# Half-array products of samples with turned keys and of the prompt with V, issued in turn on both halves of the columns

## The chip, the cores and the metric

The kernel runs on one core of one Trainium2 chip. The metric is the device time of one execution in microseconds (us). A core has engines with queues of their own, which run beside each other and wait for each other through semaphores: TensorE (PE, matrix products; its weight loads are listed as PEld), VectorE (DVE), ScalarE (ACT), GpSimd (POOL) and SyncE (SP), which here only issues transfers (DMA). TensorE is an array of 128 rows by 128 columns; the stationary operand of a product lies in the array, its columns become the output's partitions. A product with only 64 stationary columns occupies half of the columns: here called a half-array product, on half A (output partitions 0 to 63) or half B (64 to 127).

## The reference

One layer of a decoder for two groups of requests that share all weights: a prompt of 512 tokens (with 16 learned tokens ahead of it) and 8 samples of 8 new tokens, each with 1024 past tokens in a paged cache. Each layer has a state-space branch, a sparse attention branch (16 heads, 4 key/value heads of 64 elements), a gated sum of both, and a two-matrix network. All in float32. The part that matters here, cut down:

```python
def attend_selected(q, k_sel, v_sel, valid):
    qh = q.reshape(b, nq, ATT_KV_HEADS, ATT_GROUP, HEAD_DIM).astype(F32)
    s = jnp.einsum('bqhgd,bqkhd->bqhgk', qh, k_sel.astype(F32)) * HEAD_DIM ** -0.5
    s = jnp.where(valid[:, :, None, None, :], s, -jnp.inf)
    p = jax.nn.softmax(s, axis=-1)
    o = jnp.einsum('bqhgk,bqkhd->bqhgd', p, v_sel.astype(F32))

y_ssm, ssm_new, conv_new = ssm_mixer(...)            # state-space branch
y_att = attend(q, k, v, qi, wi, ki)                  # 128 (prompt) or 256 (samples) best keys
merged = sigmoid(g_ssm) * (y_ssm @ w_ssm_proj) + sigmoid(g_attn) * (y_att @ w_attn_proj)
```

The kernel does not gather the selected keys: it scores all of them and adds a mask that is very negative where a key isn't selected.

## The kernel before, in words

The stages run one after another: the normed input times w_in, with convolution and state-space scan (to about 690 us), the attention of the samples and then of the prompt (about 690 to 953 us), with the product of the state-space branch and w_ssm_proj spread among both (`L1068`), the rest of the merge, and the network. The order in which an engine's instructions stand is not the order of the source: a scheduler with a model of its own of how long things take places them; the source gives what depends on what. On TensorE it puts the products of `L1068`, and later the first of w_attn_proj (`L162`), wherever the attention is not ready. They are called fillers below.

**Samples** (`sample(b)`, 8 of them, each cut into steps by `yield` and run as a pipeline). A gather brings the sample's keys `Kg` and values `Vg` from the pages. TensorE transposes the keys (`L892`), and copies bring them from PSUM (the accumulators' memory) to `KcT`: those of the first pair of heads (hp = 0) by VectorE, those of the second (hp = 1) by ScalarE (`L893`). Then the scores (`L900`): for three stretches of keys (512, 512 and 64), one half-array product with the queries of hp = 0 on half A and one with those of hp = 1 on half B, both into one PSUM buffer `v`. VectorE adds the mask and takes the maximum (`L901`), ScalarE takes the exponential (`L904`), TensorE transposes the probabilities (`L913`, `L916`), and half-array products with V follow (`L923`, `L926`).

**Prompt** (`query(t, hp, gp)`, 16 groups: four blocks t of 128 queries, two pairs of heads hp, two halves gp). Scores (`L1002`, `L1003`), mask and maximum (`L1004`), exponential (`L1007`), scaling (`L1018`), then transposes of the probabilities (`L1024`) and copies into `PT`: of the pair's first head (e = 0) by VectorE, of the second (e = 1) by ScalarE (`L1025`). One step of the pipeline later come the products with V (`L1034`): for each of nk = t + 1 blocks of keys, one half-array product for e = 0 on half A and one for e = 1 on half B, and a full one for the first 16 keys (`L1035`).

A wait that the kernel's framework puts in is of the data: a product of hp = 0 waits for VectorE's copy, one of hp = 1 for ScalarE's. So the scheduler may place an A product as soon as VectorE's copy is expected, and its B later.

Of the kernel before, what the change touches and what calls it, by code (L numbers as in the profile page):

```python
# [1 line left out]

# [1 line left out]

# [66 lines left out]
def body(ctx, tc, a, o):  # L71
    nc = tc.nc
    SB, PS, DR = bass.MemoryType.SB, bass.MemoryType.PSUM, bass.MemoryType.DRAM
    act, dve, pool, pe, sy = nc.scalar, nc.vector, nc.gpsimd, nc.tensor, nc.sync
# [9 lines left out]
    def pst(tag):  # L84
        return psp.tile([128, 512], FT, tag=tag, name=tag, bufs=PSB[tag])

    class Pipe:
# [8 lines left out]
        def run(self, units=()):  # L96
            for u in units:
                self.push(u)
            while self.live:
                self.push()  # L100

    alt = [0]

# [76 lines left out]
    Vt = ap_.tile([128, 6, 256], FT, name="Vt")  # L180
# [45 lines left out]
    for t in range(5):  # L226
# [7 lines left out]
        for q in range(2):  # L234
            ps = mis()
            pv = ps.rearrange("p (k n) -> p k n", k=4)
# [26 lines left out]
    def pieces(n):  # L263
        return [(c, min(c + 512, n)) for c in range(0, n, 512)]
# [49 lines left out]
    with tc.tile_pool(name="p1", bufs=1, reuse_waits="tile") as p1:  # L314
# [26 lines left out]
        pv = ps.rearrange("p (k n) -> p k n", k=4)  # L341
# [202 lines left out]
        for kp in range(8):  # L544
            hp, gi = divmod(kp, 4)
# [312 lines left out]
    with tc.tile_pool(name="p2s", bufs=1, reuse_waits="tile") as p2, \  # L858
            tc.tile_pool(name="p2k", bufs=1, reuse_waits="tile") as p2k:
        qTs = p2.tile([128, 8, 64], FT, name="qTs")  # L860
        sy.dma_start(qTs, d_q[:, :, 512:576].rearrange("k p n -> p k n"))
        QZs = [p2.tile([128, 2, 64], FT, name=f"QZ{i}") for i in range(2)]
        for z in QZs:
            pool.memset(z, 0.0)
        krows = a["cache_k"].rearrange("d n (s e) h c -> (d n s) (e h c)", e=4)
        vrows = a["cache_v"].rearrange("d n (s e) h c -> (d n s) (e h c)", e=4)

        def sample(b):
            QZ = QZs[b % 2]
            for hp in range(2):  # L870
                for e in range(2):
                    src = qTs[64 * e:64 * e + 64, 4 * hp:4 * hp + 4, 8 * b:8 * b + 8]
                    dst = QZ[64 * e:64 * e + 64, hp, 32 * e:32 * e + 32].rearrange("p (g s) -> p g s", s=8)
                    act.copy(dst, src)
            Kg, Vg = [], []
            for lst, name, src in ((Kg, "Kg", krows), (Vg, "Vg", vrows)):
                for q in range(2):
                    lst.append(p2k.tile([128, 1024], FT, tag=name, name=name, bufs=4 if name == "Kg" else 2))
                    pool.indirect_dma_start(out=lst[q], out_offset=None, in_=src,
                                            in_offset=bass.IndirectOffsetOnAxis(ap=idx2[:, b, q:q + 1], axis=0))  # L880
            P = p2.tile([128, 1088], FT, tag="P", name="P", bufs=3)
            sy.dma_start(P,
                         bass.AP(tensor=d_ms.tensor, offset=d_ms.offset + (32 * (b // 2) + 8 * (b % 2)) * 1088,
                                 ap=[[0, 16], [1088, 8], [1, 1088]]))
            KcT = p2.tile([128, 2, 1024], FT, tag="KcT", name="KcT", bufs=2)
            for q in range(2):
                for hp in range(2):
                    dv = KcT[:, hp, :].rearrange("c (p s) -> c s p", s=8)
                    ps = pst("s")
                    pv = ps.rearrange("p (k n) -> p k n", k=4)  # L890
                    for i in range(4):
                        pe.transpose(pv[:, i, :], Kg[q][:, 256 * i + 128 * hp:256 * i + 128 * hp + 128], idf)  # L892
                    (act.copy if hp else dve.tensor_copy)(dv[:, 4 * q:4 * q + 4, :], pv)  # L893
            yield
            mx = p2.tile([128, 12], FT, tag="mxs", name="mxs", bufs=2)
            for c, (c0, c1) in enumerate(pieces(1088)):
                v = pst("s")[:, :c1 - c0]
                for hp in range(2):
                    kk = KcT[:, hp, c0:c1] if c < 2 else KT[:, hp, 528:592]
                    pe.matmul(v[64 * hp:64 * hp + 64], QZ[:, hp, :], kk, start=True, stop=True)  # L900
                dve.tensor_tensor_reduce(P[:, c0:c1], v, P[:, c0:c1], 1.0, NEG, OP.add, OP.max, accum_out=mx[:, c:c + 1])  # L901
            dve.tensor_scalar(mx[:, 3:4], mx[:, 0:1], mx[:, 1:2], None, op0=OP.max)
            dve.tensor_scalar(mx[:, 4:5], mx[:, 3:4], mx[:, 2:3], -0.125, op0=OP.max, op1=OP.mult)
            act.activation(P, P, AF.Exp, scale=0.125, bias=mx[:, 4:5], accum_out=mx[:, 5:6])  # L904
            dve.reciprocal(mx[:, 9:10], mx[:, 5:6])
            yield
            PTs = p2.tile([128, 9, 128], FT, tag="PTs", name="PTs", bufs=1)
            pv_ = P[:, 0:1024].rearrange("r (p s) -> r s p", s=8)
            for q in range(2):
                ps = pst("a")  # L910
                pv = ps.rearrange("p (k n) -> p k n", k=4)
                for i in range(4):
                    pe.transpose(pv[:, i, :], pv_[:, 4 * q + i, :], idf)  # L913
                (act.copy if q else dve.tensor_copy)(PTs[:, 4 * q:4 * q + 4, :], pv)
            ps = pst("a")
            pe.transpose(ps[:64, 0:128], P[:, 1024:1088], idf)  # L916
            act.copy(PTs[:64, 8, :], ps[:64, 0:128])
            py = pst("a")
            for s in range(9):
                for hp in range(2):  # L920
                    h = slice(64 * hp, 64 * hp + 64)
                    if s < 8:
                        pe.matmul(py[h, 0:128], PTs[:, s, h], Vg[s // 4][:, 256 * (s % 4) + 128 * hp:256 * (s % 4) + 128 * hp + 128],  # L923
                                  start=(s == 0), stop=False)
                    else:
                        pe.matmul(py[h, 0:128], PTs[:64, 8, h], Vt[:64, 5, 128 * hp:128 * hp + 128],  # L926
                                  start=False, stop=True)
            on = p2.tile([128, 128], FT, tag="on", name="on", bufs=2)
            dve.tensor_scalar(on, py[:, 0:128], mx[:, 9:10], None, op0=OP.mult)
            yield  # L930
            py = pst("a")
            pe.transpose(py[:, 0:128], on, idf)
            for e in range(2):
                pr = slice(64 * e, 64 * e + 64)
                src = py[pr, 0:128].rearrange("p (h x) -> p h x", h=2)[:, :, 32 * e:32 * e + 32].rearrange(
                    "p h (g s) -> p h g s", s=8)
                h_, l_ = [y[pr, :, 512 + 8 * b:520 + 8 * b].rearrange("p (h g) s -> p h g s", h=2) for y in (yah, yal)]
                act.activation(h_, src, AF.Copy)
                dve.tensor_tensor(l_, src, h_.bitcast(FT), op=OP.subtract)

        Pipe().run(sample(b) for b in range(8))
    p4s_stack = ctx.enter_context(ExitStack())
    p4s = p4s_stack.enter_context(tc.tile_pool(name="p4s", bufs=1, reuse_waits="tile", side="right"))
    with tc.tile_pool(name="p2h", bufs=1, reuse_waits="tile", side="right") as p2h, \
# [6 lines left out]
        for kv in range(4):  # L951
            hp, e = divmod(kv, 2)
# [13 lines left out]
        def query(t, hp, gp):  # L966

            L, nk = LT[t], t + 1
# [24 lines left out]
            PT = p2.tile([128, 2, 4, 2, 128], FT, tag="PT", name="PT", bufs=2)  # L993
            PR = p2.tile([96, 256], FR, tag="PR", name="PR", bufs=2)
            for g in range(2):
                P2 = p2q.tile([128, 2, 528], FT, tag="P", name="P2", bufs=3)
                mx = p2q.tile([128, 2, 6], FT, tag="mx", name="mx", bufs=4)
                for e in range(2):
                    lq = QS[:, 2 * gp + g, e, :]
                    for i, (c0, c1) in enumerate(cuts):  # L1000
                        v = pst("s")[:, :c1 - c0]
# [18 lines left out]
                for e in range(2):  # L1020
                    ps = pst("a")
                    pv = ps.rearrange("p (k n) -> p k n", k=4)
                    for j in range(nk):
                        pe.transpose(pv[:, j, :], P2[:, e, 128 * j:128 * j + 128], idf)  # L1024
                    (act.copy if e else dve.tensor_copy)(PT[:, e, :nk, g, :], pv[:, :nk, :])  # L1025
                pr_ = pst("a")
                pe.transpose(pr_[:96, 0:128], flat(ts).bitcast(FT), idf)
                act.copy(PR[:, 128 * g:128 * g + 128], pr_[:96, 0:128])
# [1 line left out]
            py = pst("s")  # L1030
            for j in range(nk):
                for e in range(2):
                    kv = 64 * (2 * hp + e)
                    pe.matmul(py[64 * e:64 * e + 64, 0:256], Vt[:, j, kv:kv + 64], PT[:, e, j], start=(j == 0), stop=False)  # L1034
            pe.matmul(py[:, 0:256], VZ[:, 128 * hp:128 * hp + 128], PR, start=False, stop=True)  # L1035
            k0 = 4 * hp + 2 * gp
            pv = py[:, 0:256].rearrange("p (g n) -> p g n", g=2)
            h_ = yah[:, k0:k0 + 2, 128 * t:128 * t + 128]
            act.activation(h_, pv, AF.Copy)
            dve.tensor_tensor(yal[:, k0:k0 + 2, 128 * t:128 * t + 128], pv, h_.bitcast(FT), op=OP.subtract)  # L1040

        Pipe().run(query(t, hp, gp) for t in range(4) for hp in range(2) for gp in range(2))

    HALVES = ((0, HQ), (HQ, NQ))
# [404 lines left out]
```

## Time and profile before

| | us |
|---|---|
| median of 3 runs (lowest to highest) | 1459.08 (1458.08 to 1460.82) |
| profiled execution | 1461.18 |
| its span, first to last instruction | 1459.4 |
| TensorE busy | 1422.9 (97%) |
| VectorE busy | 1091.1 (75%) |
| ScalarE busy | 754.3 (52%) |

A record of TensorE begins when the product begins to stream and ends when its last result is out, so records that follow each other overlap, and the sum of their durations is more than the time they took. What a group of records took is read from start to start, or from the union of their busy time in a window. Every float32 half-array product is listed as two records.

### The profile page before, as it was taken

What the parts mean: (1) busy time and instruction counts of PE and PEld (TensorE: products, weight loads), DVE (VectorE), ACT (ScalarE), POOL (GpSimd) and SP (SyncE); (2) the same over time, 40 slices, a digit from 0 to 9 for tenths busy, and PEclk for the clock granted to TensorE, in tenths of its full rate; (3) what the DMA queues carried; (4) which work ended last, traced back from release to release, by engine and by line L of the source; (5) the groups of instructions that cost most, each with busy time, mean ns of one, the idle gap of its engine ahead of it and who ended that gap; (6) DMA issues with size and microseconds to landing.
All of it is one profiled execution on the core that took longest, in us unless ns stands there. A gap on an engine that the chain in (4) does not pass through costs nothing.

```text
span 1459.4 us, 26586 instructions
## 1 busy us (share of the span) xinstructions
PE 1422.9 (97%) x9808; PEld 1271.7 (87%) x9808; DVE 1091.1 (75%) x2248; ACT 754.3 (52%) x1719; POOL 327.0 (22%) x479
## 2 busy tenths in 40 slices
PE   7999999999999999999999999999999999999998
PEld 6998999988987988889688988898798988888986
DVE  6799989999769676572645777765589887878775
ACT  5553365556655664343655777732364554435441
POOL 2110011337445345252422633100000000000001
PEclk9999999999999999999999999999999999999999
DMA  7334375787987878767974533235223222332322
GB/s 199 92 80 117 113 219 152 219 243 209 273 238 199 257 225 235 224 180 248 310 221 128 156 87 86 69 104 177 80 87 102 88 88 85 87 89 87 89 70 73
DMA packets 249340, 222.07 MB, mean 152 GB/s; under 512 B 39325, under 2 KB 212241, under 8 KB 249186
## 3 DMA queue, kind: packets, MB, share of 16 engines
q1 hardware_dynamic: 243962, 201.50, 47.7%
q0 software_dynamic: 5248, 18.88, 3.8%
q8 instruction: 77, 1.26, 0.4%
q14 instruction: 53, 0.43, 0.1%
HBM read 175.50 MB, written 44.07 MB: 150 GB/s over the span
## 4 chain that ended last, share of the span: by engine, by line
PE 83%; DMA 8%; DVE 4%; ACT 2%; POOL 1%; issue 1%; SPq 0%; POOLq 0%; DVEq 0%; ACTq 0%
PE w L162 27%; PE s L1203 15%; PE w L1068 7%; PE a L1329 6%; PE w L1329 4%; PE a L162 3%; DMA bc<-d_ac 2%; PE s L900 2%; PE s L1034 2%; PE a L1203 2%; PE s L763 2%; DMA st<-in_state_ssm_dram 1%; DMA out_dram<-st 1%; PE s L775 1%; PE a L1024 1%; PE a L923 1%
## 5 line engine op out<-in xcount | busy, mean ns | idle before, releaser
L162 PE MATMUL w<-uh,wh 128*128 128x288 f32 (+1 forms) x1168 | 355.4, 304 | 8.4 <-ACT tg L301 2.8
L162 PE MATMUL w<-ul,wh 128*128 128x288 f32 (+1 forms) x1168 | 352.8, 302 | 1.7 <-DVE ul L242 1.7
L162 PE MATMUL w<-uh,wl 128*128 128x288 f32 (+1 forms) x1168 | 353.9, 303 | 0.0
L162 PEld LDWEIGHTS w<-uh,wh 128*128 128x128 f32 x1168 | 222.1, 190 | 15.7 <-ACT tg L301 3.3
L162 PEld LDWEIGHTS w<-ul,wh 128*128 128x128 f32 x1168 | 221.9, 190 | 4.5 <-DVE ul L242 1.9
L162 PEld LDWEIGHTS w<-uh,wl 128*128 128x128 f32 x1168 | 221.2, 189 | 2.6 <-issue 1.9
L123 DVE TENSOR_TENSOR wl<-wr,wh 128x1024 fp32r<-128x1024 f32 x129 | 158.9, 1233 | 78.2 <-ACT wh L122 77.0
L122 ACT ACTIVATE wh<-wr 128x1024 fp32r<-128x1024 f32 x129 | 135.7, 1057 | 143.8 <-PE w L162 81.7
L1205 DVE TENSOR_TENSOR h<-h,s 128x512 f32<-128x512 f32 (+1 forms) x161 | 108.3, 679 | 58.7 <-PE s L1203 58.4
L1203 PE MATMUL s<-dh,hh 128*128 128x512 f32 (+1 forms) x302 | 119.0, 394 | 0.0
L1203 PE MATMUL s<-dl,hh 128*128 128x512 f32 (+1 forms) x302 | 118.7, 393 | 0.0
L172 POOL TENSOR_TENSOR rs<-rs,cst 128x1 f32<-128x1 f32 (+2 forms) x15 | 9.3, 617 | 417.4 <-DVE rs L171 417.2
L1203 PE MATMUL s<-dh,hl 128*128 128x512 f32 (+1 forms) x242 | 95.0, 392 | 0.0
L1068 PE MATMUL w<-ysh,wh 128*128 128x288 f32 x256 | 78.2, 308 | 0.2 <-DVE ms L1073 0.2
L122 ACT ACTIVATE dh<-wr 128x1024 fp32r<-128x1024 f32 x38 | 39.8, 1057 | 73.2 <-PE s L1203 59.3
L1068 PE MATMUL w<-ysh,wl 128*128 128x288 f32 x256 | 77.2, 302 | 0.0
L1068 PE MATMUL w<-ysl,wh 128*128 128x288 f32 x256 | 76.6, 300 | 0.0
L750 ACT ACTIVATE bc<-bc,acum 128x128 f32<-128x128 f32 (+1 forms) x160 | 48.9, 380 | 52.1 <-DMA bc<-d_ac 46.5
L612 DVE SCALAR_TENSOR_TENSOR ca<-rb,cwT,ca 128x616 f32<-128x616 f32 x72 | 69.5, 967 | 0.2
L1203 PEld LDWEIGHTS s<-dl,hh 128*128 128x128 f32 x302 | 56.6, 188 | 12.5
L1203 PEld LDWEIGHTS s<-dh,hh 128*128 128x128 f32 x302 | 56.7, 188 | 10.2 <-DVE h L1205 0.5
L762 DVE SCALAR_TENSOR_TENSOR bc<-bc,dts,cb 128x128 f32<-128x128 f32 (+1 forms) x160 | 54.1, 402 | 0.2
(492 smaller groups left out, 3702.9 us busy)
## 6 DMA issues: line engine op xcount, KB each, us to landing
wr<-in_w_in_dram SPq DMA_DIRECT2D x26, 1024.0 KB
wr<-in_w_up_dram SPq DMA_DIRECT2D x32, 512.0 KB
wr<-in_w_down_dram SPq DMA_DIRECT2D x32, 512.0 KB
st<-in_state_ssm_dram SPq DMA_DIRECT2D x16, 512.0 KB
bc<-d_ac SPq DMA_DIRECT2D x32, 256.0 KB
out_dram<-st SPq DMA_DIRECT2D x16, 512.0 KB
wr<-in_w_ssm_proj_dram SPq DMA_DIRECT2D x16, 512.0 KB
wr<-in_w_in_dram SPq DMA_DIRECT2D x12, 512.0 KB
```

The source lines that it names most:

```text
L122: act.activation(hi, raw, AF.Copy)
L123: (lo_eng or dve).tensor_tensor(lo, raw, hi.bitcast(FT), op=OP.subtract)
L162: pe.matmul(ps[:, :c1 - c0], p[:, k, :], x[:, c0:c1], start=(k == 0 and i == 0), stop=(k == 7 and i == 2))
L612: dve.scalar_tensor_tensor(ca[:, 0:616], rb[:, k:k + 616], cwT[:, 24 * k + ct:24 * k + ct + 1], ca[:, 0:616], op0=OP.mult, op1=OP.add)
L750: act.activation(bc[:n, i, :n], bc[:n, i, :n], AF.Relu, scale=-1.0, bias=acum[:n, c, h0 + i:h0 + i + 1])
L762: dve.scalar_tensor_tensor(mt, mt, dts[:n, c, 8 * g + hh:8 * g + hh + 1], cb[:n, :n], op0=OP.mult, op1=OP.mult)
L763: pe.matmul(py[64 * (hh % 2):64 * (hh % 2) + 64, 128 * (hh // 2):128 * (hh // 2) + n], xt[:n, 64 * hh:64 * hh + 64], mt, start=True, stop= ...
L900: pe.matmul(v[64 * hp:64 * hp + 64], QZ[:, hp, :], kk, start=True, stop=True)
L1068: pe.matmul(ps[:, :HQ], p[:, k, mc], x[k][:, c0:c1], start=(k == 0 and i == 0), stop=(k == 3 and i == 2))
L1203: pe.matmul(ps, p, w[:, cc], start=(k == 0 and i == 0), stop=(k == len(ws) - 1 and i == len(terms) - 1))
L1205: dve.tensor_tensor(h2[:, t, cc], h2[:, t, cc], ps, op=OP.add)
L1329: pe.matmul(ps, p[:, k, :], q[:, k, :], start=(k == 0 and j == 0), stop=(k == 3 and j == 2))
```

## The change

The program's products, copies and sizes stay as they are. For the products of `L900` (now `L906`) and `L1034` (now `L1044`), each one after the first is placed behind the one before it in source order (`issue_after`), so they stand on TensorE in the order A B A B; other instructions may still stand between them. And the first of each group gets a wait for the last copy (ScalarE's) beside the one it has for VectorE's (`needs`).

```diff
+    def needs(ins, other):
+        tc.add_manual_dep(ins, other.name, mybir.DependencyInfo(mybir.DependencyClass.Sync, mybir.DependencyReason.DATA), reason="pair")
...
-                    (act.copy if hp else dve.tensor_copy)(dv[:, 4 * q:4 * q + 4, :], pv)
+                    copied = (act.copy if hp else dve.tensor_copy)(dv[:, 4 * q:4 * q + 4, :], pv)
...
                 for hp in range(2):
                     kk = KcT[:, hp, c0:c1] if c < 2 else KT[:, hp, 528:592]
-                    pe.matmul(v[64 * hp:64 * hp + 64], QZ[:, hp, :], kk, start=True, stop=True)
+                    with tc.issue_after(mm.ins) if c + hp else nullcontext():
+                        mm = pe.matmul(v[64 * hp:64 * hp + 64], QZ[:, hp, :], kk, start=True, stop=True)
+                    if c + hp == 0:
+                        needs(mm.ins, copied.ins)
...
-                    (act.copy if e else dve.tensor_copy)(PT[:, e, :nk, g, :], pv[:, :nk, :])
+                    copied = (act.copy if e else dve.tensor_copy)(PT[:, e, :nk, g, :], pv[:, :nk, :])
...
-                    pe.matmul(py[64 * e:64 * e + 64, 0:256], Vt[:, j, kv:kv + 64], PT[:, e, j], start=(j == 0), stop=False)
+                    with tc.issue_after(mm.ins) if j + e else nullcontext():
+                        mm = pe.matmul(py[64 * e:64 * e + 64, 0:256], Vt[:, j, kv:kv + 64], PT[:, e, j], start=(j == 0), stop=False)
+                    if j + e == 0:
+                        needs(mm.ins, copied.ins)
```

TensorE's order before, at the scores of the fourth sample. The names carry buffer numbers: `s_8955` is the PSUM buffer of the first 512 keys, `s_8959` of the second, `s_8963` of the last 64; in each buffer the first row listed is half A, the second half B. `L1068` are fillers.

```order
L900 MATMUL s_8955<-KcT_8886,QZ1_8621 64x512
L900 MATMUL s_8959<-KcT_8886,QZ1_8621 64x512
L1068 MATMUL w_10985<-ysh_10915,wh_10939 128x288
L1068 MATMUL w_10985<-ysl_10916,wh_10939 128x288
L1068 MATMUL w_10985<-ysh_10915,wl_10938 128x288
L1068 MATMUL w_10985<-ysh_10921,wh_10939 128x288
L1068 MATMUL w_10985<-ysl_10922,wh_10939 128x288
L900 MATMUL s_8955<-KcT_8886,QZ1_8621 64x512
L900 MATMUL s_8959<-KcT_8886,QZ1_8621 64x512
L900 MATMUL s_8963<-KT_76,QZ1_8621 64x64 x2
```

The same sample after (`L906` is the line that was `L900`, `L931` and `L934` the products with V of the sample before it, `L1080` the fillers):

```order
L1080 MATMUL w_11005<-ysh_10933,wh_11001 128x288
L906 MATMUL s_8955<-KcT_8886,QZ1_8621 64x512 x2
L906 MATMUL s_8959<-KcT_8886,QZ1_8621 64x512
L931 MATMUL a_8933<-Vg_8781,PTs_8917 64x128 x8
L931 MATMUL a_8933<-Vg_8783,PTs_8917 64x128 x8
L934 MATMUL a_8933<-Vt_77,PTs_8917 64x128 x2
L906 MATMUL s_8959<-KcT_8886,QZ1_8621 64x512
L906 MATMUL s_8963<-KT_76,QZ1_8621 64x64 x2
```

The two halves of the first buffer now stand together; of the second buffer A stands ahead of the products with V and B behind them. In six of the eight samples all six products stand in a row; the fourth, shown here, and the sixth are cut like this.

TensorE's order before, at one group of the prompt with t = 1 (`PT_9996` holds its probabilities, `L1024` and `L1027` transpose those of the next group, `L1035` closes the group):

```order
L1034 MATMUL s_10194<-PT_9996,Vt_77 64x256
L1068 MATMUL w_11831<-ysl_11744,wh_11825 128x288
L1068 MATMUL w_11831<-ysh_11743,wl_11824 128x288
L1068 MATMUL w_11831<-ysh_11749,wh_11825 128x288
L1068 MATMUL w_11831<-ysl_11750,wh_11825 128x288
L1024 MATMUL a_10133<-cst_66,P2_10091 128x128 x3
L1024 MATMUL a_10138<-cst_66,P2_10091 128x128 x3
L1027 MATMUL a_10143<-cst_66,ts_10108 96x128
L1034 MATMUL s_10194<-PT_9996,Vt_77 64x256 x3
L1035 MATMUL s_10194<-PR_9997,VZ_9746 128x256
```

The same group after (`L1044` is the line that was `L1034`, `L1047` was `L1035`):

```order
L1032 MATMUL a_10133<-cst_66,P2_10091 128x128 x3
L1080 MATMUL w_11863<-ysh_11749,wh_11825 128x288
L1080 MATMUL w_11863<-ysl_11750,wh_11825 128x288
L1080 MATMUL w_11863<-ysh_11749,wl_11824 128x288
L1032 MATMUL a_10138<-cst_66,P2_10091 128x128 x3
L1044 MATMUL s_10194<-PT_9996,Vt_77 64x256 x4
L1010 MATMUL s_10230<-KS_9433,QS_10081 128x400
L1035 MATMUL a_10143<-cst_66,ts_10108 96x128
L1047 MATMUL s_10194<-PR_9997,VZ_9746 128x256
```

The group's first product has moved behind the fillers and transposes, to the other three. The fillers stand in other places all through both attention stages; up to the first sample's scores and from the last group of the prompt on, TensorE's order is the same.

## Rows read from the trace of the kernel before

**Rows 1.** The page: busy time, share of the span and instructions of TensorE.

```profile
PE 1422.9 (97%) x9808; PEld 1271.7 (87%) x9808; DVE 1091.1 (75%) x2248; ACT 754.3 (52%) x1719; POOL 327.0 (22%) x479
```

**Rows 2.** Windows over the attention stages; the first line names the columns.

```profile
core 0: us, PE busy (x) PEld busy (x) DVE busy (x) ACT busy (x) POOL busy (x), PEclk, DMA share, GB/s
700.00:720.00 20.00, 19.38 (x157) 13.94 (x157) 11.62 (x31) 13.76 (x29) 9.42 (x9) 1.00 0.95 312
780.00:800.00 20.00, 20.00 (x174) 16.65 (x171) 8.96 (x23) 10.26 (x21) 6.19 (x7) 1.00 0.47 140
...
920.00:940.00 20.00, 20.00 (x156) 17.85 (x155) 15.45 (x60) 16.11 (x38) 3.48 (x16) 1.00 0.22 67
940.00:960.00 20.00, 18.92 (x143) 15.94 (x142) 10.88 (x37) 12.44 (x30) 2.43 (x12) 1.00 0.13 38
```

**Rows 3.** Waits of TensorE, 716 to 944 us: us in total, times, longest.

```profile
PE w L1068 <- DVE ms L1073: 0.2, 1, 0.2
```

**Rows 4.** Groups by line, TensorE, 683 to 953 us: busy us, mean ns, idle before.

```profile
L1068 PE MATMUL w<-ysh,wh 128*128 128x288 f32 x256 | 78.2, 308 | 0.2 <-DVE ms L1073 0.2
...
L1034 PE MATMUL s<-PT,Vt 128*64 128x256 f32 x160 | 28.2, 391 | 0.6 <-DVE yal L1040 0.3 <-DVE PT L1025 0.2
```

**Rows 5.** Windows of line L1034 alone: us, PE busy (records), PEld, clock, DMA.

```profile
822.00:823.00 1.00, 0.64 (x2) 0.19 (x2) 1.00 0.00 0
856.00:858.00 2.00, 1.08 (x6) 0.47 (x6) 1.00 0.68 187
940.00:943.00 3.00, 1.95 (x16) 1.06 (x16) 1.00 0.01 3
```

**Rows 6.** Timeline of TensorE at a lone product: start us, length us, instruction.

```profile
854.79 0.65 PE L1034 MATMUL s<-PT,Vt 128*64 128x256 f32 x2
855.37 0.41 PE L1068 MATMUL w<-ysh,wh 128*128 128x288 f32 x1
```

**Rows 7.** Timeline of TensorE at two fillers.

```profile
788.12 0.30 PE L1068 MATMUL w<-ysh,wh 128*128 128x288 f32 x1
788.26 0.29 PE L1068 MATMUL w<-ysl,wh 128*128 128x288 f32 x1
```

**Rows 8.** Windows of line L900 alone, one for each sample, columns as in rows 5.

```profile
694.00:699.00 5.00, 3.45 (x12) 1.34 (x12) 1.00 0.88 293
701.00:707.00 6.00, 3.95 (x12) 1.22 (x12) 1.00 0.96 349
713.00:717.00 4.00, 2.34 (x12) 1.45 (x12) 1.00 0.93 343
724.00:731.00 7.00, 3.98 (x12) 1.22 (x12) 1.00 0.79 291
737.00:746.00 9.00, 4.14 (x12) 1.19 (x12) 1.00 0.90 274
753.00:762.00 9.00, 4.47 (x12) 1.31 (x12) 1.00 0.69 211
768.00:772.00 4.00, 3.12 (x12) 0.95 (x12) 1.00 0.24 82
779.00:788.00 9.00, 4.57 (x12) 1.20 (x12) 1.00 0.16 48
```

**Rows 9.** Timeline at the first sample: its first scores, ScalarE's last copy.

```profile
695.09 2.05 PE L900 MATMUL s<-KcT,QZ 128*64 128x512 f32 x5 [0.83 <-DVE KcT L893]
695.33 1.11 ACT L893 COPY KcT<-s 128x512 f32<-128x512 f32 x1
```

**Rows 10.** Timeline of ScalarE: a copy of the largest PT.

```profile
949.00 0.59 ACT L1025 COPY PT<-a 128x512 f32<-128x512 f32 x1
```

**Rows 11.** Timeline of TensorE at the fourth sample's B products.

```profile
727.68 0.64 PE L900 MATMUL s<-KcT,QZ 128*64 128x512 f32 x1
727.69 0.33 PE L900 MATMUL s<-KT,QZ 128*64 128x64 f32 x2
728.16 1.45 PE L900 MATMUL s<-KcT,QZ 128*64 128x512 f32 x3
```

More of the change, by code (lines that the diff above doesn't have):

```diff
@@ L1 @@
-from contextlib import ExitStack
+from contextlib import ExitStack, nullcontext
 import numpy as np
```

## The prediction, made before the changed kernel had run

> **What bounds the kernel now.** I read the page first: TensorE (PE) is busy 97% of the span [rows 1]. Then the table of windows over the two attention stages, about 695 to 953 us: from 780 to 940 us PE is busy for the whole of each 20 us shown, at full clock (1.00), while VectorE and ScalarE have 3.9 to 11 us of every 20 free; only at either end (700 to 720, 940 to 960) is there a gap [rows 2]. The reader is to see there that a microsecond of PE work saved between 716 and 944 us is a microsecond of the kernel, unless another engine is late. The list of waits says the same: in those 228 us PE itself waited 0.2 us for anybody [rows 3]. What it does meanwhile is seen in the groups by line: 768 products of the SSM projection (L1068, in three forms of 256), which need nothing of the attention and fill every hole, and among them the half-array products, of L1034 (prompt probabilities with V, 160 records) [rows 4] and of L900 (scores of samples). Record lengths overlap, so I price by windows of one line's union of busy time, and by start to start, not by mean lengths.
>
> **What a half-array product costs alone, and in a pair.** Every fp32 half-array product shows as two records. Two records by themselves take 0.64 us, six (one pair, one product alone) 1.08, and sixteen (eight products, four pairs, issued A B A B) 1.95 [rows 5]. From 1.08 to 1.95 lie ten records. If a slot holds either a pair or one product alone, the six records are two slots and the sixteen four: (1.95 - 1.08) / 2 = 0.435 us a slot, and 0.64 + 0.435 = 1.08 fits. So a pair takes what one product takes: the two halves of the columns run side by side at full speed, in this very kernel. A product that stands alone between full-array work costs 855.37 - 854.79 = 0.58 us from its start to the start of the next instruction [rows 6]; the 0.15 over a slot is the way in and out. A filler product takes 788.26 - 788.12 = 0.13 to 0.14 us [rows 7].
>
> **Part 1, prompt with V (L1034, 16 query groups).** Before, in 11 of the 16 groups (4 of t = 0, 4 of t = 1, 3 of t = 2) the scheduler has put the first A product some instructions ahead of its B. The piece of PE's order for one group of t = 1 shows it: one product, then fillers and transposes, then three. After, that group's four stand in a row, and so it is in 13 groups. Two keep one product apart (a transposition stands between A and B, which B can't share), and one more is cut between two pairs, which costs the 0.15 only. Saved: (11 - 2) x 0.58 - 0.15 = 5.1 us. The five groups that were whole already, all of t = 3 among them, gain nothing.
>
> **Part 2, sample scores (L900, 8 samples of 4 large and 2 small products).** The windows give 3.45, 3.95, 2.34, 3.98, 4.14, 4.47, 3.12 and 4.57 us per sample [rows 8]. The third is what fully paired products cost (two large slots, 2.34 with a late partner); the seventh, with one large product alone, costs 3.12. After, PE's order has A B A B A B whole in six samples and A B A, other work, B A B in the fourth and the sixth. I set 2.34 for the six, 3.12 for the two. The windows of the sixth and eighth hold other half-array products inside, so I count them as 4.0, like their neighbours. Sample by sample:
> - first: 3.45 - 2.34 = 1.1 saved, but the first product now waits for ScalarE's copy, which ends at 695.33 + 1.11 = 696.44, while PE began at 695.09 [rows 9], and nothing stands ahead of it that could be done meanwhile: 1.35 lost, together -0.2;
> - second: 1.6, of which I take half (0.8), since PE is not full around there (19.38 of 20 us) and the DMA engines are at 0.95 [rows 2], so that what follows may be late;
> - third 0; fourth 3.98 - 3.12 = 0.9; fifth 4.14 - 2.34 = 1.8; sixth 4.0 - 3.12 = 0.9; seventh 3.12 - 2.34 = 0.8; eighth 4.0 - 2.34 = 1.7.
>
> Sum 6.7 us. Its ends: 2 us, if only the fifth and the eighth gain (3.5) and the first one's wait stands (1.35), and 11, if every sample gains in full and no wait shows (the eight windows add up to 30.0; 30.0 - 6 x 2.34 - 2 x 3.12 = 9.7) and A and B, which now start together, save another 0.2 in each of the six.
>
> **The waits that are added.** The first product of each group now waits for ScalarE's copy as well as VectorE's; behind it in PE's queue stands everything else, fillers too. In the prompt, PE's order after the change has 21 to 51 instructions between the transposes for ScalarE's copy and the pair in the first 14 groups, and 6 and 1 in the last two, just as before; 21 fillers are 2.8 us against a copy of 0.59 [rows 10], so the fillers cover this wait and it costs nothing. For the second and third sample 9 and 10 instructions stand in it (the transposes of the probabilities), for the other five 25 and more. Only the first sample is bare, and it is in the sum. Uncovered, a wait would cost up to 1.35 us at a sample and 0.59 at a prompt group.
>
> **What is given back at the end.** The fillers are a fixed number. Around the last query group of t = 2 the order has 27 fillers (9 of L1080, and 18 of L166, which is the new number of L162) where before it had 35: 8 x 0.14 = 1.1 us less cover in a stretch where ScalarE is the next busiest engine (16.1 of 20 us) and PE begins to show gaps (18.92 of 20) [rows 2]. I count that as lost; its ends are 0 and 3 us (were ScalarE to bound the last four groups).
>
> Sum: 5.1 + 6.7 - 1.1 = 10.7, about 11 us. Against the profiled execution (span 1459.4, 1461.2 in all) that is 1450; this execution lay 2.1 us above the median of the three runs, 1459.1, so the forecast for the median is **1448 us**. Nothing outside 690 to 960 us moves: PE's order is the same up to there and after.
>
> **A rule of the Trainium skill, weighed.** In the fourth sample the small product of the A half, last but one in the program, starts at 727.69, 0.01 us after the first record of B, and ahead of B's other three large records at 728.16 [rows 11]. So here PE runs the two halves past each other when their data is there, and the third sample got its pairs though its program order was A A B B A B. The Trainium skill ("TensorE: Matmul & The Clock Gate", Part 3: Packing small matmuls) says that matmuls start and end strictly in program order. The trace does not agree. By that rule the third sample would have needed a third large slot before and would gain one now, 2 x 0.43 = 0.9 us more, and the sum would be 11.6, 1447.5 us; that is inside the forecast's own case, so it gets no chance of its own.
>
> **Rivals.**
> - *PE overtakes anyway, so the order is not what separates the halves, and the change does not do what it says.* For it: the third sample. Against it: in 11 prompt groups B stands 5 to 23 instructions behind A, with full-array products between, and A's price there is that of one alone. Time: 1459.
> - *Only the prompt's part is kept.* The sample stage is paced by the gathers of K and V (DMA 0.95 early on) and what PE saves turns into waits for them. Against it: from 780 us on DMA is below half and PE waits for nothing. Time: 1459.1 - 5.1 = 1454.
> - *Slower: the wait for both copies.* If the covers fail, every group's first product holds up the whole PE queue: 8 x 1.35 + 16 x 0.59 = 20.2 us, against the sum without the first sample's wait, 10.7 + 1.35 = 12.1: 1459.1 + 20.2 - 12.1 = 1467. It decides from a mean wait of 12.1 / 24 = 0.5 us a group. Against it: the instruction counts above.
>
> **How the numbers follow.** Forecast (8 to 16 us gained) 0.66; only the prompt or about that 0.17; no change 0.08; slower 0.07; more than 16 us 0.02. The upper end of gain is 5.1 + 11 = 16 us, 1443; the range's other end is 1456, a gain of 3, which leaves out no change and slower. This measurement can tell about 0.2%, 2.9 us, from no change. Faster: 0.66 + 0.02 + nearly all of 0.17 = 0.83; same 0.08 + 0.02 = 0.10; slower 0.07.
>
> **What would show it.** In the profile after: the prompt's line in windows at 0.64, 1.08, 1.51 or 1.95 us for whole groups with no lone pair of records but in two groups; its total over the stage about 5 us less; the samples' windows at 2.1 to 2.4 us, two near 3.1; no wait of PE for KcT or PT over 0.5 us but in the first sample; the fillers ending some 10 us earlier. It is wrong if PE shows idle time ahead of these lines that adds up to 5 us, or if the last four groups stretch.

## The result, and the profile after

| us | before | after |
|---|---|---|
| median of 5 runs each (lowest to highest) | 1459.08 (1457.99 to 1460.82) | 1452.2 (1450.71 to 1454.46) |
| span of the profiled execution | 1459.4 | 1452.7 |

The ratio is 0.9944 (95% interval 0.9932 to 0.9957): 6.9 us, or 0.56%, faster. The forecast was 1448, a gain of 11. The time lies in the range of 1443 to 1456, but some 4 us of the expected gain are missing.

The page's line of engines, as in [rows 1]:

```profile
PE 1407.2 (97%) x9808; PEld 1268.0 (87%) x9808; DVE 1089.0 (75%) x2248; ACT 755.7 (52%) x1719; POOL 331.5 (23%) x479
```

TensorE is busy for 15.7 us less, and the span is only 6.7 us shorter: TensorE stands idle for some 9 us more, 6.5 of them in the attention stages (the account below). Busy time is a union of records that overlap, so it is a sign, not the account.

First what was saved. The sample scores, one window a sample, as in [rows 8] (us, PE busy (records), PEld, clock, DMA share, GB/s):

```profile
696.00:700.00 4.00, 3.24 (x12) 1.31 (x12) 0.66 0.92 316
704.00:707.00 3.00, 2.01 (x12) 0.77 (x12) 1.00 0.81 279
715.00:719.00 4.00, 2.05 (x12) 0.77 (x12) 1.00 0.88 251
728.00:736.00 8.00, 3.12 (x12) 0.94 (x12) 1.00 1.03 316
740.00:745.00 5.00, 2.05 (x12) 0.77 (x12) 1.00 0.72 234
753.00:763.00 10.00, 3.12 (x12) 0.94 (x12) 1.00 0.70 235
766.00:770.00 4.00, 2.05 (x12) 0.77 (x12) 1.00 0.40 130
780.00:784.00 4.00, 2.00 (x12) 0.83 (x12) 1.00 0.57 176
```

The two cut samples take 3.12 us, as forecast, the whole ones 2.0 to 2.05 (forecast 2.34, or 0.2 less if A and B start together). Together it is 19.6 us, where it was 30.0. The first one stands out: 3.24 us at a clock of 0.66, where the others have 1.00.

The same for the prompt's line, against [rows 5]:

```profile
827.00:828.00 1.00, 0.65 (x4) 0.20 (x4) 1.00 0.48 133
941.00:946.00 5.00, 1.90 (x16) 1.06 (x16) 1.00 0.21 59
```

A pair alone (four records) takes 0.65 us; before, one product alone (two records) took 0.64. That is the price on which the forecast stood.

Then what was given back. The waits of TensorE, 716 to 944 us, as in [rows 3] (us in total, times, longest):

```profile
PE a L940 <- DVE on L937: 2.3, 1, 2.3
PE w L1080 <- DVE ms L1085: 0.8, 2, 0.7
PE s L906 <- ACT KcT L897: 0.4, 1, 0.4
PE s L1010 <- DVE yal L1052: 0.3, 1, 0.3
PE s L1044 <- DVE yal L1052: 0.3, 1, 0.3
```

Before, the only row was 0.2 us. The new 2.3 us aren't ahead of the changed products: the transposition of the seventh sample's result `on` waits for VectorE. Ahead of this window a second new row stands, a transposition of probabilities that waits for ScalarE's exponential (at 703 us):

```profile
PE a L921 <- ACT P L912: 1.1, 1, 1.1
```

TensorE's timeline at the first sample, against [rows 9], and at this second pause (start, length, instruction, idle before):

```profile
693.83 0.49 PE L896 MATMUL s<-cst,Kg 128*128 128x128 f32 x3
696.59 3.03 PE L906 MATMUL s<-KcT,QZ 128*64 128x512 f32 x8 [2.27 <-ACT KcT L897]
...
785.28 0.29 PE L1080 MATMUL w<-ysh,wl 128*128 128x288 f32 x1
787.89 0.33 PE L940 MATMUL a<-cst,on 128*128 128x128 f32 x1 [2.32 <-DVE on L937]
...
789.82 0.45 PE L1080 MATMUL w<-ysh,wh 128*128 128x288 f32 x1
790.06 0.45 PE L1080 MATMUL w<-ysl,wh 128*128 128x288 f32 x1
```

The pause ahead of the first sample is 2.27 us, where it was 0.83: the 1.4 us that were forecast. But behind either pause the fillers or products run slower: at 790 us fillers start 0.24 us apart, not 0.13 to 0.14 [rows 7]. The granted clock there is 0.5 (1.2 GHz, full being 2.4) for 3.4 us from 789.5, and for 3.4 us from 697.3; the kernel before had no drop in this stage. In the windows, as in [rows 2] (us, busy PE, PEld, DVE, ACT, POOL, then PE clock, DMA share, GB/s), the first row from before, the others after:

```profile
680.00:700.00 20.00, 18.10 (x124) 15.38 (x124) 8.18 (x13) 7.72 (x15) 1.87 (x2) 1.00 0.91 326
```

```profile
680.00:700.00 20.00, 16.74 (x115) 14.44 (x114) 6.99 (x8) 6.91 (x11) 1.88 (x2) 0.93 0.92 330
700.00:720.00 20.00, 17.86 (x151) 13.35 (x152) 12.46 (x35) 13.98 (x32) 8.53 (x8) 0.98 0.95 298
780.00:800.00 20.00, 17.53 (x142) 15.04 (x139) 9.49 (x24) 6.18 (x13) 4.44 (x5) 0.91 0.51 169
920.00:940.00 20.00, 19.38 (x150) 16.20 (x150) 13.38 (x63) 19.00 (x47) 4.12 (x21) 1.00 0.08 23
940.00:960.00 20.00, 18.90 (x143) 17.42 (x143) 11.21 (x24) 7.76 (x17) 0.81 (x4) 1.00 0.27 78
```

From 780 to 800 us TensorE was busy for 20.00 of 20 us [rows 2], and now for 17.53, at a mean clock of 0.91.

Why is `on` late? The timelines of VectorE, ScalarE and SyncE's queue (SPq) around that pause, after:

```profile
779.04 1.51 DVE L127 TENSOR_TENSOR ysl<-yw,ysh 128x576 fp32r<-128x576 f32 x1 [2.48 <-ACT ysh L126]
...
781.72 0.69 DVE L909 CUSTOM_DVE_ANT_0 P<-s,P 128x512 f32<-128x512 f32 x1
...
786.82 0.76 DVE L127 TENSOR_TENSOR ysl<-yw,ysh 128x576 fp32r<-128x576 f32 x1 [3.62 <-ACT ysh L126]
787.49 0.35 DVE L937 TENSOR_SCALAR on<-a,mxs 128x128 f32<-128x128 f32 x1
...
783.50 0.69 ACT L126 ACTIVATE ysh<-yw 128x576 fp32r<-128x576 f32 x1 [3.10 <-DMA yw<-d_y]
786.10 0.68 ACT L126 ACTIVATE ysh<-yw 128x576 fp32r<-128x576 f32 x1 [1.91 <-DMA yw<-d_y]
...
780.58 0.81 SPq L1063 DMA_DIRECT2D yw<-d_y  x2
```

And VectorE's before:

```profile
787.86 0.35 DVE L929 TENSOR_SCALAR on<-a,mxs 128x128 f32<-128x128 f32 x1
...
789.04 0.76 DVE L123 TENSOR_TENSOR ysl<-yw,ysh 128x576 fp32r<-128x576 f32 x1 [0.32 <-ACT ysh L122]
...
794.20 0.76 DVE L123 TENSOR_TENSOR ysl<-yw,ysh 128x576 fp32r<-128x576 f32 x1 [0.33 <-ACT ysh L122]
```

`ysl` and `ysh` are the two parts of `yw`, which later fillers multiply. Before, `on` stood ahead of both of VectorE's `ysl`. After, the scheduler has both ahead of it: VectorE stands still for 3.62 us, since ScalarE's `ysh` waits for the transfer of `yw`, and `on`, whose data have been there since about 783.2, stands behind. The transfer itself was issued at 780.58, once the conversions ahead of it (VectorE's at 779.04 took until 780.55) were done with the two buffers of `yw`. So the path is transfer, ScalarE, VectorE, `on`, TensorE, and no instruction on it belongs to a line that was edited.

### The profile page after: what moved, and what is told of

Read it like the earlier page. It is cut to its first block, busy times and chain, and to the rows that moved or that the text cites. A ratio compares the mean times of both kernels' runs of the same rounds, so it can differ in the third digit from the quotient of the medians.

```text
span 1452.7 us, 26579 instructions
## 1 busy us (share of the span) xinstructions
PE 1407.2 (97%) x9808; PEld 1268.0 (87%) x9808; DVE 1089.0 (75%) x2248; ACT 755.7 (52%) x1719; POOL 331.5 (23%) x479
## 4 chain that ended last, share of the span: by engine, by line
PE 80%; DMA 9%; DVE 4%; ACT 3%; issue 1%; POOL 1%; SPq 1%; POOLq 0%; DVEq 0%; ACTq 0%
PE w L166 28%; PE s L1215 15%; PE w L1080 6%; PE a L1341 6%; PE w L1341 4%; PE a L166 3%; DMA bc<-d_ac 2%; PE s L1044 1%; PE s L767 1%; PE a L1215 1%; PE s L906 1%; PE a L1032 1%; PE s L779 1%; PE a L710 1%; DMA d_x<-tk 1%
## 5 line engine op out<-in xcount | busy, mean ns | idle before, releaser
L1080 PE MATMUL w<-ysh,wh 128*128 128x288 f32 x256 | 79.5, 313 | 0.9 <-DVE ms L1085 0.8
L1080 PE MATMUL w<-ysl,wh 128*128 128x288 f32 x256 | 77.8, 304 | 0.2 <-POOL ysl L127 0.2
L1080 PE MATMUL w<-ysh,wl 128*128 128x288 f32 x256 | 77.5, 303 | 0.0
L616 DVE SCALAR_TENSOR_TENSOR ca<-rb,cwT,ca 128x616 f32<-128x616 f32 x72 | 66.4, 924 | 0.2
```

What stands on the lines that cost most here:

```text
L616: dve.scalar_tensor_tensor(ca[:, 0:616], rb[:, k:k + 616], cwT[:, 24 * k + ct:24 * k + ct + 1], ca[:, 0:616], op0=OP.mult, op1=OP.add)
L1080: pe.matmul(ps[:, :HQ], p[:, k, mc], x[k][:, c0:c1], start=(k == 0 and i == 0), stop=(k == 3 and i == 2))
```

## The account of the stage

To compare kernels I use one stretch: from the start of the first transposition of a sample's keys to the start of the last prompt product with V. In it, "idle" is the time in which no TensorE instruction runs; "samples" and "prompt" are the times from the start of each such half-array product to the start of the next instruction, idle taken out; "other" is the rest.

| one profiled execution each, us | stage | idle | samples | prompt | other | starts of clock drops |
|---|---|---|---|---|---|---|
| before | 270.3 | 2.3 | 27.1 | 26.0 | 215.0 | none |
| after | 262.9 | 8.8 | 17.9 | 20.7 | 215.6 | 697.3, 789.5 |
| after, once more (e9) | 262.8 | 8.7 | 18.2 | 20.7 | 215.2 | 695.2, 787.4 |
| e1 prompt only | 264.4 | 3.0 | 27.1 | 20.7 | 213.6 | none |
| e2 samples only | 269.5 | 9.9 | 18.3 | 24.3 | 217.1 | 696.3, 788.4 (6.8 us) |
| e3 first sample as before | 265.4 | 10.6 | 19.5 | 20.7 | 214.7 | 719.9, 795.0 |
| e4 `ysl` behind `on` | 257.8 | 7.1 | 16.7 | 20.7 | 213.4 | none |
| e4 once more | 258.6 | 6.7 | 17.7 | 20.7 | 213.6 | 696.6 |
| e6 order without the wait | 270.6 | 5.4 | 23.3 | 25.7 | 216.2 | none |
| e8 extra work in the first pause | 264.4 | 10.1 | 16.7 | 20.7 | 217.1 | 787.9 |
| e11 three `yw` | 257.3 | 6.8 | 16.9 | 20.7 | 213.0 | 697.7 |
| e11 once more | 256.6 | 6.1 | 17.7 | 20.7 | 212.1 | 697.9 |
| e12 three `yw`, `ysl` behind `on` | 258.7 | 8.0 | 17.5 | 20.5 | 212.7 | 698.3 |
| e13 samples only, three `yw` | 260.3 | 5.4 | 17.2 | 24.3 | 213.5 | 696.6 |

After against before: prompt -5.3, samples -9.2, idle +6.5, other +0.6, together -7.4; what lies outside the stage moved by 0.7 (1189.1 and 1189.8). The three kernels that were profiled twice agree within 0.8 us on the stage, so it tells more than whole times, which in the experiments scattered by 3 to 13 us from lowest to highest of one kernel. Not every profile is of a typical execution, though: those of after, e2, e3 and the first e4 are of the longest of their runs, e2's 6.1 us and e3's 4.4 above the median.

## The experiments

Theory A: the edit saves some 14.5 us on TensorE and gives 7 back, for the most part in two pauses, each with some us at the lower clock. The rivals: the samples' part brings nothing, because transfers pace its stage; and, for each pause, another cause. Ratios are to the kernel before on the same chip.

**e1, prompt only; e2, samples only.** In each, the other line is written as before:

```diff
-    with tc.issue_after(mm.ins) if ... else nullcontext():
-        mm = pe.matmul(...)
-    if ... == 0:
-        needs(mm.ins, copied.ins)
+    pe.matmul(...)
```

> The prompt's products are paired as in the changed kernel, the samples' products are issued as before, without the wait for both copies. Theory A (the samples' part gains about 9 us on TensorE, and gives some 7 back in two pauses of TensorE, each followed by a few us at the lower clock): only the prompt's gain of 5.3 us is left, 1459.1 - 5.3 = 1454, no drop of the granted clock near 697 or 789 us, and no TensorE wait for VectorE's `on` over 1 us. Rival (the samples' part brings nothing, its stage is paced by transfers): about the time of the changed kernel, 1452.

> The samples' products are paired and wait for both copies, the prompt's are issued as before. Theory A: VectorE's order around 785 us is that of the changed kernel, so both pauses and both clock drops stay: 1459.1 - 9.2 + 3.1 + 4.3 = 1457.3. Rival one (the samples' part brings nothing or costs): 1459 or more. Rival two (the samples' gain is whole, and it is the prompt's part that falls short): 1452 or less.

e1: 1453.26, 0.9933 (0.9917 to 0.9949). e2: 1454.66, 0.9946 (0.9931 to 0.9961). The times can't tell the theories apart: the intervals of e1, e2 and after overlap. Nor do they bear out theory A's sizes: it had a gain of about 5 us for e1 and 2 for e2, and the intervals give at least 7 and 5. By the times each part alone gains about as much as both together; why, no run shows. The profiles tell where the pauses come from. Longest waits of TensorE over the stage, e1:

```profile
PE s L905 <- DVE KcT L897: 1.3, 2, 0.8
PE s L1041 <- ACT PT L1030: 0.6, 1, 0.6
```

and e2:

```profile
PE a L940 <- DVE on L937: 3.8, 1, 3.8
PE s L906 <- ACT KcT L897: 2.8, 2, 2.3
```

Both pauses and both drops come with the samples' part, as theory A has it. With e1 at 264.4 and after at 262.9, that part added only 1.5 us of gain to the prompt's in the stage. How much it gains alone, e2's profile does not say: with a pause of 3.8 us, a drop twice as long and an execution 6 us above the median, its 269.5 is likely high.

**e3, the first sample as before.** Neither wait nor order for b = 0:

```diff
-    with tc.issue_after(mm.ins) if c + hp else nullcontext():
+    with tc.issue_after(mm.ins) if b and c + hp else nullcontext():
...
-    if c + hp == 0:
+    if b and c + hp == 0:
         needs(mm.ins, copied.ins)
```

> The changed kernel, but the first of the eight samples neither waits for both copies nor is put in turn. Theory A: the pause of 2.54 us ahead of its products is 1.1 us again as before, the clock stays at full speed there, and its products take 3.4 us instead of 3.2, since the pairs are lost too: 1452.2 - 1.4 (wait) - 1.5 (the lower clock on what follows) + 0.2 = about 1449.5. Rival (the drop of the clock at 697 us has nothing to do with the pause): the drop stays, 1452.2 - 1.4 + 1.2 = 1452.

1455.08, 0.9945 (0.9926 to 0.9964), the ratio of after; the stage, in a long execution, is 2.5 us longer than after's. The first pause is 0.83 us again and has no drop behind it, but the third sample now waits, and a drop follows there (719.9). TensorE in e3:

```profile
717.61 0.54 PE L1080 MATMUL w<-ysh,wh 128*128 128x288 f32 x2 [1.80 <-ACT ysh L126]
717.99 0.27 PE L924 MATMUL a<-cst,P 128*64 128x128 f32 x1
720.43 1.98 PE L906 MATMUL s<-KcT,QZ 128*64 128x512 f32 x4 [2.17 <-ACT KcT L897]
```

So my expectation of 1449.5 failed, and not for the rival's reason: the wait moved one step down the pipe of samples. Between the second and the third sample's scores only 14 fillers stand here, and one of them waited 1.80 us itself, for ScalarE's `ysh`. That nothing can be won at the first samples is not shown by this one run.

**e4, the conversions behind `on`** (run twice):

```diff
...
-    split(yw, ysh[-1], ysl[-1], (pool, dve)[k % 2])
+    with tc.issue_after(turned[0].ins) if k in (8, 9) else nullcontext():
+        split(yw, ysh[-1], ysl[-1], (pool, dve)[k % 2])
```

`turned[0]` is the last sample's `on`.

> The changed kernel, but the two conversions of the next stage's yw (ysh, ysl; k = 8 and 9) that VectorE and ScalarE took ahead of the last samples' `on` are issued behind it. Theory A: TensorE no longer waits 2.3 us for `on` at 785 us, the clock does not drop at 789 us: 1452.2 - 4.3 = 1448. Rival (the pause only moves, to where the later conversions are needed, or `on` is late by itself, behind ScalarE's exponential): 1451 to 1453.

> The changed kernel with the two conversions behind `on`, once more, to be compared with the changed kernel on the same chip. Theory A: 4 to 5 us below it, ratio to the kernel before about 0.991. Rival (the 0.9915 of its first run was luck of the chip): within 2 us of the changed kernel.

1449.83, 0.9915 (0.9901 to 0.9929), and 1449.96, 0.9931 (0.9916 to 0.9946). VectorE in the first e4:

```profile
786.21 0.35 DVE L939 TENSOR_SCALAR on<-a,mxs 128x128 f32<-128x128 f32 x1
797.22 0.35 DVE L939 TENSOR_SCALAR on<-a,mxs 128x128 f32<-128x128 f32 x1 [0.99 <-PE a L936]
797.49 0.75 DVE L127 TENSOR_TENSOR ysl<-yw,ysh 128x576 fp32r<-128x576 f32 x1
```

The second pause and its drop are gone in both (0.7 us of wait, for ScalarE's exponential, is left near there), and the stage is 4 to 5 us shorter than after's 262.9: theory A's 4.3. The first e4 has no drop at the first sample either, so the second, 4.3 shorter, is the fairer comparison. The rival, a pause that only moves, falls by the stage. The times alone would not settle it: beside the changed kernel on one chip (e9, next) the second e4 is 2.5 us faster by the medians, not the 4 to 5 expected, and the intervals overlap.

**e9, the changed kernel again,** unedited, on the chip of the next three.

> The changed kernel itself once more, on the chip and beside the runs of the next three. Theory A: the two TensorE pauses (about 2.3 us each, ahead of the first sample's products and ahead of the turn of `on` near 785 us) are in this execution too, each with a drop of the granted clock behind it. Time as before, ratio 0.993 to 0.996. If the pauses are chance of one execution: they are missing or elsewhere.

1452.46, 0.9946 (0.9929 to 0.9963). Both pauses (2.26 and 2.61 us) and both drops are there again: they belong to the kernel.

**e6, the order without the wait**: both calls of `needs` are left out.

> The products are put in turn (A B A B), but the first of a group does not wait for both copies. The instruction order then still has the first A product alone in nearly all prompt groups and in most samples, some instructions ahead of its B. If the wait is what makes the pairs, and a product alone costs about 0.58 us: no gain, 1458 to 1461, at TensorE waits as small as before (2.3 us of idle time over the stage). If putting them in turn is what makes the pairs: about the time of the changed kernel or better, 1447 to 1452, since the waits are gone.

1461.92, 1.0023 (1.0006 to 1.0040): slower than before, if anything. Without the wait the scheduler again places the first A ahead, and only the rest of the group stands in turn. In the prompt it is the wait that makes the pairs (25.7 us, before 26.0). In the samples order alone saves 3.8 of the 9.2 us (27.1 to 23.3), but idle time rises by 3.1 us and the rest by 1.2, where I had expected waits as small as before. VectorE's order in e6 has the seventh `on` ahead of both `ysl`, as before, so it is also the wait, by way of the scheduler, that moved VectorE's instructions.

**e8, work in the first pause**: ten more transpositions into the score tile that the products then overwrite.

> The changed kernel with ten extra 128 x 128 transposes of 0.125 us into the score tile of the first sample, which is written again by the products right behind them; so TensorE is at work for 1.25 us of its pause of 2.3 us there, and the products start no earlier. Theory A (a pause of over 2 us is what brings the clock down): no drop near 697 us, the first sample's products take 2.0 us instead of 3.2; the drop near 789 us stays. 1452 - 1.7 = 1450.5. Rival (the drop there comes whatever TensorE does): it stays, 1452.

1453.16, 0.9948 (0.9925 to 0.9970). TensorE in e8:

```profile
692.86 1.31 PE L904 MATMUL s<-cst,Kg 128*128 128x128 f32 x10 [0.39 <-ACT KcT L897]
694.75 1.94 PE L909 MATMUL s<-KcT,QZ 128*64 128x512 f32 x8 [0.58 <-issue]
```

The transpositions start 0.11 us apart. With the pause cut into 0.39 and 0.58 us the drop behind it is gone, as theory A has it, though this is one run, and the first e4 had no drop there without such work. The samples' products take 16.7 us in both kernels, not 17.9: the drop at the first sample costs 1.2 us by this line alone. But no time was won, and my 1450.5 failed. The pause at `on` is 3.3 us here, not 2.3, since ScalarE gets the second `yw` 6.5 us after the first of the two transfers was issued, not 5.5, and a pause of 1.3 us for ScalarE's `ysh` at 711 us is new. Why both came, this run doesn't show.

**e11, three buffers for `yw`** (run twice); **e12, the same and `ysl` behind `on`; e13, the same and samples only:**

```diff
-    yw = p4s.tile([128, NQ], FT, tag="yw", name="yw", bufs=2)
+    yw = p4s.tile([128, NQ], FT, tag="yw", name="yw", bufs=3)
```

> The changed kernel with three buffers for yw in place of two, so that the transfer for the second of VectorE's two conversions can start one turn earlier; VectorE's order, with both conversions ahead of the last but one sample's `on`, stays. Theory A (the pause near 785 us is a wait for yw's transfer, passed on through ScalarE's ysh and VectorE's ysl to `on`, which stands behind them): the pause goes or is under 1 us, the clock does not drop there, and the stage from the first sample's transposes to the last prompt product shrinks from 262.8 to 258 to 260 us; time 1448 to 1450. Rival (`on` is late because VectorE or ScalarE are busy by then, not for the transfer): pause and drop stay, stage 262 to 263, time 1452.

> The changed kernel with three buffers for yw, once more. Theory A: the stage from the first sample's transposes to the last prompt product is 257 to 258.5 us again, without a pause or a drop of the clock near 785 us; time 1445 to 1449, ratio 0.990 to 0.993. If its first 1445.9 was luck of the executions: about the time of the changed kernel, 1451 to 1453.

> Three buffers for yw, and the two conversions issued behind `on` as well. Theory A: the two edits take away one and the same pause, so together they bring no more than either: stage 257.5 to 259.5 us, time 1448 to 1450. If each takes away a wait of its own: stage 254 to 256, time 1445.

> Only the samples' products paired, the prompt's issued as before, with three buffers for yw. Theory A: the samples' part is worth what it saves on TensorE (about 9 us) less the first samples' waits (about 3 us of idle and a drop of the clock), once the pause near 785 us is gone: stage 262 to 264 us against 269.5 with two buffers, time 1452 to 1454. Rival (the samples' part brings nothing by itself, its stage is paced by transfers): stage 268 to 270.

e11: 1445.85, 0.9907 (0.9888 to 0.9926), and 1448.17, 0.9915 (0.9894 to 0.9935). VectorE in the first e11:

```profile
783.09 0.76 DVE L127 TENSOR_TENSOR ysl<-yw,ysh 128x576 fp32r<-128x576 f32 x1 [0.68 <-ACT ysh L126]
...
785.01 0.34 DVE L937 TENSOR_SCALAR on<-a,mxs 128x128 f32<-128x128 f32 x1
```

`ysl` still stands ahead of `on`, but waits 0.68 us, not 3.62; TensorE's pause and the drop near 789 are gone, and the stage is 257.3 and 256.6. So the pause needs both, the transfer that comes late and the order that lets it reach `on`; taking away either one removes it. The stage is 5.5 to 6.3 us shorter than the changed kernel's, more than the pause and its drop; the two were not run side by side on one chip. e12: 1451.39, 0.9941 (0.9919 to 0.9962). Its stage, 258.7, agrees with both edits removing the same pause, but it has waits of its own, 0.7 to 1.0 us each at 802, 817 and 820 us. Why its time lies 3 to 6 us above e11's, with a stage only 1.4 to 2.1 longer, stays open.

e13: 1448.67, 0.9918 (0.9901 to 0.9935), stage 260.3. Without the second pause the samples' part and the third buffer are worth 10.0 us of stage (270.3 to 260.3), more than I expected; the samples' products themselves take 9.9 us less. So the rival that transfers of K and V pace this stage falls. What a third buffer does to the kernel before, no run shows; before, the waits for `yw` didn't reach TensorE.

## Why the prediction was right in direction and short in size

- **A pair costs what one product costs: right.** 0.65 us for a pair, 0.64 before for one product.
- **Part 1, prompt: right.** Forecast 5.1, measured 5.3 us (26.0 to 20.7), and the same in nearly every kernel that has this edit.
- **Part 2, samples: right in what the products cost.** The windows add up to 19.6 us, at the full clock in the first one to 18.4; the forecast gave 6 x 2.34 + 2 x 3.12 = 20.3.
- **"The waits that are added": this step failed.** It counted what stands on TensorE between copy and product, and said "Only the first sample is bare, and it is in the sum." For the products' own waits that nearly held: outside the first sample the longest are 0.56 us, at the last prompt group, and 0.42 at the third sample. Its sign of being wrong, 5 us of idle time ahead of the changed lines, did not show (3.6 us, before 1.8), because it watched those lines alone. But idle time rose by 6.5 us. Of it the sum had the first sample's 1.35 (measured 1.4) and 0.8 as half of the second sample's gain (measured 0.8, most of it the wait for the exponential at 703 us). It did not have 2.3 us ahead of `on`, because I compared TensorE's order with the order before and not VectorE's, which the same edit had rearranged, nor the half clock behind both pauses: 1.2 us in the first sample (e8), and, by estimate, 1.5 behind the second (3.4 us at 0.24 us a filler are 14 fillers, 0.11 us late each). 2.3 + 1.2 + 1.5 = 5.0 us unpriced; e4 and e11, which take away the second pause with its drop, give back 4.2 to 6.3 of stage. Another 2 us of idle time are short waits, at the third sample, at 808 us and in the last prompt groups.
- **What is given back at the end: 0.6 us.** 1.1 us were set for the last groups. From 920 us to the end of the stage TensorE was idle for 1.2 us, before for 0.55. What lies behind the stage is as before within the repeats (504.6 to 507.2 us).
- **The sum.** Forecast 10.7; 5.3 + 9.2 - 6.5 - 0.6 = 7.4 in the stage. The shortfall of 3.3 is less than what went unpriced because the samples' products, at full clock, saved 10.4 us where the forecast had 8.8, and because 1.1 us for the end stood in the sum. So the nearness of 1448 to 1452 is in part luck: two errors of opposite sign. The rule weighed for the third sample, 0.9 us more, did not come out: its window went from 2.34 to 2.05.
- **The rivals.** "PE overtakes anyway" falls: samples and prompt are both cheaper. "Only the prompt's part is kept" gave 1454 and came nearly true in the number (the samples' part added 1.5 us of stage), but not by its mechanism: the samples' products got cheaper, and their gain went into two pauses and drops of the clock. "Slower, by the wait for both copies" had the right kind of cost, idle TensorE, at 6.5 / 24 = 0.27 us a group, against the 0.5 from which it would decide.

## What to carry to other kernels

An added wait is a change to the order on every engine, if a scheduler sets it: compare the orders of the engines that feed the bottleneck as well, and look there for an instruction that waits for a transfer and now stands ahead of one that the bottleneck needs. Where a step that was saved doesn't show in the end time, list the bottleneck's idle time before and after: here one new row of 2.3 us named the place, and with a third buffer, far from the edit, the gain was nearly double (13.5 and 14.0 us, where the changed kernel had 6.9 and 7.6). Price a pause of TensorE with the slower stretch behind it, not by its length alone.

## What the runs showed of the hardware

- The kernel before has its 0.8 us pause ahead of the first sample and no drop of the clock. e8 has pauses of 1.3 us at 699 and 711 us and no drop there either. In the profiles of this study fifteen pauses of 2.2 to 3.8 us stood in this stage; at fourteen of them the granted clock fell to 0.5 (1.2 GHz), from 0.5 us before the pause's end to 1.6 us after it, for 3.4 us, once for 6.8. Behind one, of 2.27 us (the first e4), it stayed at 1.00. Where extra work cut such a pause in two, no drop followed (e8, one run).
- Two half-array products that start together lie 6 to 7 ns apart in the records. A pair of the 128 x 512 score products (two records each) takes 0.86 us from its start to the start of the next (705.900 to 706.759 in the second sample), what one such product alone takes (before, 728.588 to 729.446 in the fourth).
